# Attention scores by matmuls over 128 rows only: a two-layer encoder trunk on one Trainium2 core

## The chip, the cores and the metric

The program runs on one core of one Trainium2 chip. The core has a matmul engine (TensorE, PE in the profile, with its weight loads as PEld), three engines for elementwise work (VectorE or DVE, ScalarE or ACT, GpSimd or POOL), a queue that issues most of the transfers (SyncE, SP), and 16 DMA engines. The metric is device time in microseconds (us) from the first to the last instruction of the program; lower is better.

## The reference, cut to what matters

The input is a sequence of 2,048 tokens with 1,024 features, float32. Two layers follow each other. The first has two attentions side by side: a dilated one (A, 8 heads of 64 features) and a differential one (B, 4 heads, each with two score matrices, over all positions). The second has a banded grouped-query attention (C, 16 query heads, 4 key heads, keys within 128 positions).

```python
def differential_attention(q1, q2, k1, k2, v, lam, lam_init, subln_g):
    ...
        def attn(q, k):
            qs = lax.dynamic_slice_in_dim(q, start, Q_BLOCK, axis=2)
            s = jnp.einsum('bhqd,bhkd->bhqk', qs, k, preferred_element_type=jnp.float32) * scale + bias
            return jax.nn.softmax(s, axis=-1)

        a = attn(q1, k1) - lam * attn(q2, k2)
        return jnp.einsum('bhqk,bhkd->bhqd', a, v32)
...
def even_mixer(h, w_in, w_out, lq1, lk1, lq2, lk2, subln_g, lam_init):
    ...
    proj = h @ w_in
    ...
    return (y * jax.nn.silu(g)) @ w_out
```

A layer is: norm, `h @ w_in`, attention, a gate, `@ w_out`. All products are to be as good as float32.

## The kernel before, in words

**Two parts.** The matmuls take a rounded format, float32r. To keep float32's accuracy each operand is split into a high part and a low part that together hold it, and a product is the sum of high x high, high x low and low x high (`three`, three matmuls of 128 rows). Scores are products over the 64 features of a head, so 128 rows hold both parts of one operand at once. `scores` uses that: its first matmul, over 128 rows, has q's high and low part in the two halves and k's high part in both halves, and gives (q high + q low) k high. Its second, over the 64 rows where q's high part lies, adds q high x k low. The two write one PSUM tile, one right behind the other where nothing comes between. The columns of one matmul are keys: 512 in B, 256 or 512 or 384 in A, 384 (256 at the ends) in C.

**Stages.** In order: projections for B (`layer0_proj`); differential attention (`diff_head`, one call to a head, 8 steps of two query blocks of 128); dilated attention (`dil_pair`, two heads of 64 features to a pair; each head is done in the tokens' order, `dil_natural`, and by residue class mod 4, `dil_classes`); the first layer's output projection, run together with the second layer's first block; banded attention (`attend`, one call to a block of 128 queries, 16 in all), between which the second layer's projections lie; the second layer's gate and output projection.

**Fill.** Projections that are due later are written down as filling work beside the attentions: those of A (tiles `pp_a`, `pn_a`) beside B, the first layer's gate (`pp_g`) beside B and A, part of its output projection (`po0b`) beside A, the second layer's projections and gate (`pp_l`, `pn_l`, `pp_g`) beside C. Which instruction stands where on an engine is decided when the program is built, by a scheduler that runs its own estimate of the program; the engines then keep that order. So an edit to `scores` can shift the whole order.

**Names of the scores' tiles.** PSUM `pq` (B), `pqn` and `pqc` (A, natural and by class), `pqC` (C). Parts of k: `kBh` (high, both halves) and `kBl` (low) in B; `kn`/`kln`, `kc`/`klc` in A; `khC`/`klC` in C. After the scores VectorE adds the distance term and takes the maximum (lines 599, 777, 828, 1102), ScalarE takes the exponential, PE transposes, ScalarE and VectorE split the result in two parts (lines 626 and 627 in B), and PE multiplies by v (`py`, `pyn`, `pyc`, `pyC`).

**Queues.** Loads stand in SP's queue in the scheduler's order. A load into a buffer waits there until the buffer's last reader is done, and what is behind it waits as well. The tiles of v in C have 5 buffers (`vC`, tag `v`), k's high and low parts 2 each.

Of the kernel before, what the change touches and what calls it, by code (L numbers as in the profile page):

```python
# [37 lines left out]
def rsqrt(nc, pool, out, xin, name, iters=3):  # L38
    """out = xin ** -0.5 on VectorE: a first guess from the exponent, then Newton steps."""
# [18 lines left out]
class Bufs:  # L58
    """A pool with each tag's number of buffers."""
# [10 lines left out]
def tile_encoder(ctx: ExitStack, tc: tile.TileContext, x, c, ada_w, ada_b, norm_g, ab_w_in, ab_w_out,  # L70
# [38 lines left out]
    # ---------------------------------------------------------------- constants  # L109
# [12 lines left out]
    def small_consts(pool, ps):  # L122
        """Conditioning vector, lambda and the per-head norm's weights."""
# [28 lines left out]
    def ada_acc(pool, l, c0, name, raw=None):  # L152
        """Columns c0 .. c0 + 512: the sum over a partition's features of silu(c) * ada_w."""
# [19 lines left out]
    def ada_bias(ps, l):  # L173
        """ada_b's three parts and norm_g, a feature to a partition."""
# [42 lines left out]
    def ada_load(tiles, l, j):  # L217
        """The scale's and the shift's columns of ada_w to tiles[i][j], [128, KC, 512]."""
        for i in (1, 0):
            for n in range(2):  # L220
                c0, ks = i * D + j * 512, slice(n * KC // 2, (n + 1) * KC // 2)
                nc.sync.dma_start(tiles[i][j][:, ks],
                                  ada_w[l, :, c0:c0 + 512].rearrange("(k p) f -> p k f", p=P)[:, ks])

    # ---------------------------------------------------------------- norm + transposes
# [9 lines left out]
    def norm_block(pool, ps, l, b, xts, h):  # L235
        """512 tokens, normalised, to the features' layout: h[part][k] is [128, 512]."""
# [9 lines left out]
    def modulate(pool, l, name, src, k, h):  # L246
        """The conditioning's scale and shift, and the split into high and low parts."""
# [6 lines left out]
    # ---------------------------------------------------------------- input projections  # L254
    CH = 256

    def load_w(pool, w, c0, n, name, tag, eng=nc.vector):
        """Columns c0 .. c0 + n of w as high and low parts."""
# [12 lines left out]
    def three(pt, l, r, k, nk, after=None):  # L271
        """pt += (l0 + l1)^T (r0 + r1), less the product of the low parts."""
# [7 lines left out]
    def proj_T(pool, ps, w, c0, n, h, name, sink, wt, tick, blocks=range(TB)):  # L280
        """(h w)^T for columns c0 .. c0 + n (n <= CH), in pieces of 128 features x 512 tokens."""
# [10 lines left out]
    def proj_N(pool, ps, w, cols, n, h, name, sinks, tick):  # L292
        """h w for the n columns from each of cols, in pieces of 128 tokens x n features, block by block."""
# [12 lines left out]
    def proj_block(pool, ps, w, h, b, pieces, name, after=lambda b, n: None):  # L306
        """A block of 512 tokens by pieces of w: (first column, sink, None), 128 columns for (h w)^T,
        or (first column, None, sink), 256 columns for h w. h[part][k] is [128, 512]."""
# [27 lines left out]
    def split(pool, src, name, scale=1.0, shape=None):  # L336
        """The high and low parts of scale * src (in PSUM)."""
# [10 lines left out]
    def sink_heads(pool, dst, scale, name, classes=None):  # L348
        """A pair of 64-feature heads to dst(part, block), [128, 512]; classes(part): also by residue mod 4."""
# [13 lines left out]
    def pair(dst, h):  # L363
        """The parts of heads h and h + 1, a feature to a row."""
        return lambda i: dst[i, h:h + 2].rearrange("h f s -> (h f) s")
# [4 lines left out]
    def load_parts(q, src, h, cols, parity):  # L370
        """Head h's high parts to the first half of q and its low parts to the second, or the other way round."""
# [12 lines left out]
    def sink_v(pool, dst, dv, name, eng=nc.sync):  # L384
        """Heads of dv features, their high and low parts side by side."""
# [8 lines left out]
    # ================================================================ layer 0: norm, projections  # L394
    def load_x(pool, b, tag=None):
        """512 tokens; a tile to a pair of 128, or all in one of the tag's."""
# [23 lines left out]
    def layer0_proj(pool):  # L420
        with sbuf("pH", side="right") as hpool, psum("ps0", side="right") as ps0:
# [22 lines left out]
            # the first block waits in the second's place for the conditioning  # L444
# [9 lines left out]
            # what else is due, by the time passed in products (units of 128 x 128 x 256 x 24)  # L454
# [78 lines left out]
    # ================================================================ layer 0: differential attention  # L533
    def diff_attention(fill, psf, poolc):
        with sbuf("pB", side="right") as pool, psum("psB", side="right") as ps_:
            ps = Bufs(ps_, s=2, t=2, y=1)
            # -|k - q| by k - q; a head's slope (a power of two) is in q's scale and the exponential's
# [12 lines left out]
    NQ = 2                                            # query blocks that share a pass over V  # L550
    PB = 6

    def scores(ps_, q, kh, kl, a):
        """ps_ = q^T k less the product of the low parts; kh is in both halves, kl in half a."""
        first = nc.tensor.matmul(ps_, q, kh, start=True, stop=False)  # L555
        nc.tensor.matmul(ps_, q[a * 64:(a + 1) * 64], kl[a * 64:(a + 1) * 64], start=False, stop=True)  # L556
# [5 lines left out]
    def diff_head(pool, poolc, ps, h, ndist):  # L562
        def load_q(tp):
            q = pool.tile([P, 2, NQ * P], FR, name=f"q{h}_{tp}", tag="q", bufs=2)
            for a in range(2):
                load_parts(q[:, a], qB, 2 * h + a, slice(tp * NQ * P, (tp + 1) * NQ * P), a)
# [3 lines left out]
        KL = poolc.tile([P, S], FR, name=f"kBl{h}", tag="y2", bufs=1)  # L570
        KH = []
        for a in range(2):
            kt = pool.tile([P, S], FR, name=f"kBh{h}_{a}", tag="kh", bufs=2)
            for j in range(2):
                nc.sync.dma_start(f32(kt)[j * 64:(j + 1) * 64], kB[0, 2 * h + a])
            nc.sync.dma_start(f32(KL)[a * 64:(a + 1) * 64], kB[1, 2 * h + a])
# [669 lines left out]
```

## Time and profile before

| | |
|---|---|
| runs of the kernel before | median 3259.53 us of 3 (3256.40 to 3263.93) |
| the profiled execution, span | 3262.4 us |
| PE busy (matmuls) | 3110.2 us, 95% of the span, 14,992 matmuls |
| weight loads busy | 2323.1 us, 71% |
| DVE busy | 1915.4 us, 59% |
| ACT busy | 1494.5 us, 46% |
| POOL busy | 1141.3 us, 35% |
| transfers | 574.35 MB, mean 176 GB/s; the main queue's packets took 57.9% of 16 engines' span |
| mean granted TensorE clock | 0.968 of 2.4 GHz |

A matmul's row shows when it starts and a length whose end is modelled: successive matmuls overlap, so a busy PE need not be at its peak, and what tells the pace is the distance from one start to the next. "64\*128" in a row is the part of the array that the matmul uses, rows by columns; "64x512" is its moving operand.

### The profile page before, as it was taken

To read this page: it belongs to the slowest core of one execution; us is meant where nothing else is said; L and a number is where in the kernel's file an instruction comes from. 1 tells how busy PE (TensorE), PEld (TensorE's weight loads), DVE (VectorE), ACT (ScalarE), POOL (GpSimd) and SP (SyncE) were. 2 spreads that over 40 slices of the span, in tenths; PEclk is the share of its full clock that TensorE was granted. 3 is DMA by queue.
4 is the path that set the end of the run, shared out by engine and by line. 5 is a ranking of instruction groups with operands and counts; after the bars stand their busy time and mean duration, and the time that the engine had idled before them with its cause. 6 is when DMAs were issued, how large, how long until landed. Compare 5 with 4: busy or idle time off the path is not lost. (4 is left out here: it accounts for less than half of the span.)

```text
span 3262.4 us, 43544 instructions
## 1 busy us (share of the span) xinstructions
PE 3110.2 (95%) x14992; PEld 2323.1 (71%) x14992; DVE 1915.4 (59%) x4128; ACT 1494.5 (46%) x2841; POOL 1141.3 (35%) x755
## 2 busy tenths in 40 slices
PE   5999899999999999999999999799999999999998
PEld 4789667767767667677676776678767677777786
DVE  7434265665656656656565677653556665556476
ACT  4211245444544445444555666322456665555321
POOL 3200165454453544331242433232334343233221
PEclk8999799999999999999998999899999999999999
DMA  6677532542443444135867886686968666775654
GB/s 247 237 271 240 171 117 75 160 148 68 140 130 113 147 127 156 55 109 145 227 169 211 209 230 188 208 286 221 239 178 224 179 150 180 184 203 161 198 186 158
DMA packets 536246, 574.35 MB, mean 176 GB/s; under 512 B 31361, under 2 KB 406874, under 8 KB 529370
## 3 DMA queue, kind: packets, MB, share of 16 engines
q1 hardware_dynamic: 524186, 554.80, 57.9%
q10 hardware_dynamic: 11840, 16.78, 1.5%
q8 instruction: 118, 1.93, 0.3%
q14 instruction: 102, 0.84, 0.1%
HBM read 394.97 MB, written 176.46 MB: 175 GB/s over the span
## 5 line engine op out<-in xcount | busy, mean ns | idle before, releaser
L605 ACT ACTIVATE s<-s,nm 128x2048 f32<-128x2048 f32 x128 | 256.6, 2004 | 142.4 <-DVE nm L604 137.2
L626 ACT ACTIVATE th<-pt 128x512 fp32r<-128x512 f32 x256 | 148.2, 595 | 285.8 <-PE pt L622 247.8
L556 PE MATMUL pq<-kBl,q 64*128 64x512 f32 x512 | 259.5, 508 | 6.0 <-DMA kBl<-kB 6.0
L611 POOL TENSOR_SCALAR s<-s,rr 128x1536 f32<-128x1536 f32 x64 | 123.5, 1930 | 397.5 <-DVE rr L609 352.3
L627 DVE TENSOR_TENSOR tl<-pt,th 128x512 fp32r<-128x512 f32 x256 | 172.1, 686 | 146.3 <-ACT th L626 145.0
L555 PE MATMUL pq<-kBh,q 128*128 128x512 f32 x512 | 246.5, 482 | 7.6 <-DVE mx L599 5.6
L1102 DVE CUSTOM_DVE_ANT_0 sC<-pqC,tabC,isl 128x384 f32<-128x384 f32 (+1 forms) x256 | 150.8, 598 | 173.7 <-PE pqC L556 128.4
L599 DVE CUSTOM_DVE_ANT_0 s<-pq,ndist 128x1024 f32<-128x1024 f32 x128 | 156.3, 1221 | 159.7 <-PE pq L556 118.2
L614 POOL TENSOR_TENSOR s<-s,s 128x1536 f32<-128x1536 f32 x64 | 226.1, 3532 | 5.2
L599 DVE CUSTOM_DVE_ANT_0 s<-pq,ndist,mx 128x1024 f32<-128x1024 f32 x128 | 163.8, 1280 | 60.1 <-PE pq L556 58.4
L556 PEld LDWEIGHTS pq<-kBl,q 64*128 64x128 f32 x512 | 95.6, 188 | 138.2 <-issue 130.1
L1110 ACT ACTIVATE sC<-sC,nmC 128x384 f32<-128x384 f32 (+1 forms) x256 | 150.8, 592 | 58.3 <-DVE nmC L1107 58.1
L555 PEld LDWEIGHTS pq<-kBh,q 128*128 128x128 f32 x512 | 98.0, 192 | 89.9 <-issue 77.6
L276 PE MATMUL py<-tl,vB 128*128 128x256 f32 x512 | 155.6, 304 | 1.2 <-DVE tl L627 1.2
L622 PE MATMUL pt<-ident,s 128*128 128x128 f32 x1024 | 151.9, 275 | 2.5 <-DVE tl L627 2.5
L273 PE MATMUL py<-th,vB 128*128 128x256 f32 x512 | 151.2, 295 | 0.1
L315 POOL TENSOR_TENSOR wt_g<-wr_g,wt_g 128x1024 fp32r<-128x1024 f32 x32 | 76.8, 2400 | 199.5 <-ACT wt_g L314 196.8
L277 PE MATMUL py<-th,vB 128*128 128x256 f32 x512 | 145.7, 285 | 0.0
L1123 POOL TENSOR_SCALAR hC<-rC 128x512 fp32r<-128x512 f32 x64 | 40.1, 627 | 291.2 <-ACT rC L1122 269.8
L945 POOL TENSOR_TENSOR yr<-yr,gr 128x512 f32<-128x512 f32 (+1 forms) x46 | 59.5, 1297 | 209.5 <-DMA yr<-yT 58.9
L1116 PE MATMUL ptC<-ident,sC 128*128 128x128 f32 x736 | 131.9, 278 | 0.1
L273 PE MATMUL pp_l<-h1T,wt_l 128*128 128x512 f32 x320 | 129.1, 405 | 0.7 <-DVE vc L390 0.6
(415 smaller groups left out, 9244.3 us busy)
## 6 DMA issues: line engine op xcount, KB each, us to landing
wr_a<-in_ab_w_in_dram SPq DMA_DIRECT2D x48, 512.0 KB
wr_l<-in_c_w_in_dram SPq DMA_DIRECT2D x48, 512.0 KB
hD<-h0T SPq DMA_DIRECT2D x8, 2048.0 KB
aw_ss<-in_ada_w_dram SPq DMA_DIRECT2D x32, 512.0 KB
hs_a<-hD SPq DMA_DIRECT2D x16, 1024.0 KB
wr_g<-in_ab_w_in_dram SPq DMA_DIRECT2D x32, 512.0 KB
hs_g<-hD SPq DMA_DIRECT2D x16, 1024.0 KB
G<-gg_g SPq DMA_DIRECT2D x64, 256.0 KB
```

Of the source, the lines that this page charges most:

```text
L273: first = nc.tensor.matmul(pt, l[0], r[0], start=(k == 0), stop=False)
L276: nc.tensor.matmul(pt, l[0], r[1], start=False, stop=False)
L555: first = nc.tensor.matmul(ps_, q, kh, start=True, stop=False)
L556: nc.tensor.matmul(ps_, q[a * 64:(a + 1) * 64], kl[a * 64:(a + 1) * 64], start=False, stop=True)
L599: nc.vector.tensor_tensor_reduce(out=s_[:, half * 1024:(half + 1) * 1024], in0=pq, in1=ndist[:, o:o + 1024], scale=1.0, scalar=LOW if half ...
L605: nc.scalar.activation(s_, s_, AF.Exp, bias=nm, scale=slope_B(h), accum_out=lsum[:, a, t:t + 1])
L614: nc.gpsimd.tensor_tensor(Pm[0][:, W:], Pm[0][:, W:], Pm[1][:, W:], op=OP.add)
L622: nc.tensor.transpose(pt[:, kk, j], A[j][:, kb * P:(kb + 1) * P], ident)
L626: nc.scalar.activation(hi, src, AF.Copy)
L627: nc.vector.tensor_tensor(lo, src, f32(hi), op=OP.subtract)
L1102: nc.vector.tensor_tensor_reduce(out=s_[:, :n], in0=pq[:, :n], in1=tab[:, o:o + n], scale=1.0, scalar=isl[:, h:h + 1], op0=OP.add, op1=OP.max,
L1110: nc.scalar.activation(Sx[r][:, :n], Sx[r][:, :n], AF.Exp, bias=nm[:, h:h + 1], scale=slope_C(h), accum_out=ls[:, h:h + 1])
```

## The change: what it does

`scores` takes both operands of both matmuls from its caller, and both matmuls run over 128 rows. One operand of a pair holds its two parts in the two halves, the other is loaded to both halves, once with its high part and once with its low part. The two matmuls thus give all four products of the parts (before: three).

- B: k holds both parts in one tile (`kB`, high in the first half, low in the second; one tile to each of a head's two score matrices, one of them in a buffer of tag `kh`, which has 1 now, the other where `kBl` was). q is loaded twice, high part to both halves and low part to both halves (`q` has twice the size). The two matmuls of a pair have different weights and the same moving operand.
- A and C: q keeps its two parts in the halves; k's low part is loaded to both halves as its high part was. The two matmuls have the same weights. `klC` has twice the size, v in C 4 buffers for 5.

```diff
-    def scores(ps_, q, kh, kl, a):
-        """ps_ = q^T k less the product of the low parts; kh is in both halves, kl in half a."""
-        first = nc.tensor.matmul(ps_, q, kh, start=True, stop=False)
-        nc.tensor.matmul(ps_, q[a * 64:(a + 1) * 64], kl[a * 64:(a + 1) * 64], start=False, stop=True)
+    def scores(ps_, q0, k0, q1, k1):
+        first = nc.tensor.matmul(ps_, q0, k0, start=True, stop=False)
+        nc.tensor.matmul(ps_, q1, k1, start=False, stop=True)
         return first
...
-            q = pool.tile([P, 2, NQ * P], FR, name=f"q{h}_{tp}", tag="q", bufs=2)
+            q = pool.tile([P, 2, 2, NQ * P], FR, name=f"q{h}_{tp}", tag="q", bufs=2)
...
+                for j in range(2):
+                    nc.sync.dma_start(f32(q)[j * 64:(j + 1) * 64, a], qB[:, 2 * h + a, :, cols].rearrange("i f s -> f i s"))
...
+            kt = (pool.tile([P, S], FR, name=f"kB{h}_{a}", tag="kh", bufs=1) if a == 0 else
+                  poolc.tile([P, S], FR, name=f"kB{h}_{a}", tag="y2", bufs=1))
+            for i in range(2):
+                nc.sync.dma_start(f32(kt)[i * 64:(i + 1) * 64], kB[i, 2 * h + a])
...
-            nc.sync.dma_start(f32(KL)[mine, o:o + k1 - k0], kA[0][1, h, :, k0:k1])
+                nc.sync.dma_start(f32(KL)[j * 64:(j + 1) * 64, o:o + k1 - k0], kA[0][1, h, :, k0:k1])
...
-                    scores(pq[:, j], Q[:, c0:c0 + P], KH[:, c0:c0 + 256], KL[:, c0:c0 + 256], e)
+                    scores(pq[:, j], q, KH[:, c0:c0 + 256], q, KL[:, c0:c0 + 256])
...
-            nc.sync.dma_start(f32(KL)[mine], kA[1][1, h, :, cols])
+                nc.sync.dma_start(f32(KL)[j * 64:(j + 1) * 64], kA[1][1, h, :, cols])
...
-                V[u] = pool.tile([P, C_KV, P], FR, name=f"vC_{u}", tag="v", bufs=5)
+                V[u] = pool.tile([P, C_KV, P], FR, name=f"vC_{u}", tag="v", bufs=4)
...
-        KL = pool.tile([P, C_KV // 2, 384], FR, name=f"klC{t}", tag="kl", bufs=2)
+        KL = pool.tile([P, C_KV, 384], FR, name=f"klC{t}", tag="kl", bufs=2)
...
-                nc.sync.dma_start(f32(KL)[half, :, dst], kC[b][1, a::2, :, src].rearrange("h f s -> f h s"))
+                nc.sync.dma_start(f32(KL)[half, :, dst], kC[b][1, :, :, src].rearrange("h f s -> f h s"))
...
-                last = scores(pq[:, :n], Q[:, h], KH[:, kv, :n], KL[:, kv // 2, :n], kv % 2)
+                last = scores(pq[:, :n], Q[:, h], KH[:, kv, :n], Q[:, h], KL[:, kv, :n])
```

The scheduler's order shifts with it. On PE, in the dilated stage of the kernel before, at the scores of the fifth head's second class (`pqc_1_2`), matmuls of the gate's projection (`pp_g_3_7`) stand between the scores, the transposes (`ptc`) and the products with v (`pyc`):

```order
L273 MATMUL pp_g_3_7_18454<-hs_g_3_0_1_18198,wt_g_3_7_18451 128x512
L276 MATMUL pp_g_3_7_18454<-hs_g_3_1_1_18202,wt_g_3_7_18451 128x512
L555 MATMUL pqc_1_2_15176<-kc_1_15157,qc_1_15154 128x512
L556 MATMUL pqc_1_2_15176<-klc_1_15160,qc_1_15154 128x512
L277 MATMUL pp_g_3_7_18454<-hs_g_3_0_1_18198,wt_g_3_7_18451 128x512
L273 MATMUL pp_g_3_7_18454<-hs_g_3_0_1_18198,wt_g_3_7_18451 128x512
L276 MATMUL pp_g_3_7_18454<-hs_g_3_1_1_18202,wt_g_3_7_18451 128x512
L840 MATMUL ptc_0_3_15138<-ident,scl_0_1_15086 128x128
L840 MATMUL ptc_0_3_15138<-ident,scl_0_2_15092 128x128
```

At the same scores of the same head PE's order of the change has no filling work (line numbers are 2 higher in the changed file):

```order
L556 MATMUL pqc_1_0_15190<-kc_1_15182,qc_1_15179 128x384
L556 MATMUL pqc_1_1_15196<-kc_1_15182,qc_1_15179 128x512
L557 MATMUL pqc_1_0_15190<-klc_1_15183,qc_1_15179 128x384
L557 MATMUL pqc_1_1_15196<-klc_1_15183,qc_1_15179 128x512
L856 MATMUL pyc_0_15128<-ch_0_1_15134,vc_0_15102 128x512
L556 MATMUL pqc_1_2_15202<-kc_1_15182,qc_1_15179 128x512
L557 MATMUL pqc_1_2_15202<-klc_1_15183,qc_1_15179 128x512
L842 MATMUL ptc_0_3_15163<-ident,scl_0_1_15111 128x128
L842 MATMUL ptc_0_3_15163<-ident,scl_0_2_15117 128x128
```

Counted over the whole orders: between the first `pqn` and the last `pyc`, the order before has 384 matmuls of `pp_g` and 192 of `po0b`; the changed one has 72 of `pp_g`, of which 24 beside the first head, 24 in the last and 24 at its very end, and none of `po0b`. Of the others, 96 `pp_g` stand earlier, beside B, and 216 `pp_g` and all 192 `po0b` stand behind the last `pyc`. At that place PE's order before goes straight from the last products of the dilated stage to the output projection (`po`):

```order
L276 MATMUL po0b_1_18819<-wol0b,yh0b_4_18825 128x512
L277 MATMUL po0b_1_18819<-woh0b,yl0b_4_18826 128x512
L854 MATMUL pyc_3_17223<-ch_3_3_17262,vc_3_17197 128x384
L854 MATMUL pyc_3_17223<-cl_3_3_17263,vc_3_17197 128x384
L273 MATMUL po_0_0_18911<-woh0b,yh_0_4_18918 128x512
L276 MATMUL po_0_0_18911<-wol0b,yh_0_4_18918 128x512
```

and the changed one to what is left of the gate's projection:

```order
L856 MATMUL pyc_3_17275<-ch_3_3_17314,vc_3_17249 128x384
L856 MATMUL pyc_3_17275<-cl_3_3_17315,vc_3_17249 128x384
L273 MATMUL pp_g_2_7_18218<-hs_g_2_0_0_17960,wt_g_2_7_18215 128x512
L276 MATMUL pp_g_2_7_18218<-hs_g_2_1_0_17964,wt_g_2_7_18215 128x512
L277 MATMUL pp_g_2_7_18218<-hs_g_2_0_0_17960,wt_g_2_7_18215 128x512
```

On SP, the loads of the second block of banded attention stand in the same order in both; the kernel before loads k's low part for two heads to a half:

```order
L1077 DMA vC_20781<-vC_82 128x512
L1086 DMA khC_20783<-kC_78 64x4x384
L1087 DMA klC_20784<-kC_78 64x2x384
L1086 DMA khC_20783<-kC_78 64x4x384
L1087 DMA klC_20784<-kC_78 64x2x384
L1089 DMA qC_20785<-qC_74 64x16x128 x2
```

and the change for all four:

```order
L1079 DMA vC_20833<-vC_82 128x512
L1088 DMA khC_20835<-kC_78 64x4x384
L1089 DMA klC_20836<-kC_78 64x4x384
L1088 DMA khC_20835<-kC_78 64x4x384
L1089 DMA klC_20836<-kC_78 64x4x384
L1091 DMA qC_20837<-qC_74 64x16x128 x2
```

The order before changes between 64 and 128 rows 2,024 times, the changed one never.

## Rows read from the trace of the kernel before

**Rows 1.** Windows by stage: B, A, C (us; busy by engine, PEclk, DMA share, GB/s)

```profile
370.00:1504.00 1134.00, 1115.69 (x5477) 790.22 (x5478) 682.16 (x1248) 530.27 (x716) 518.61 (x231) 0.98 0.39 118
1504.00:2068.00 564.00, 536.67 (x2520) 391.08 (x2519) 378.79 (x986) 334.44 (x833) 190.78 (x186) 0.94 0.75 200
2315.00:3033.00 718.00, 710.92 (x3299) 519.19 (x3300) 420.43 (x1031) 411.24 (x949) 255.79 (x196) 0.98 0.70 187
```

**Rows 2.** PE's waits in B, longest in total first

```profile
PE pq L556 <- DMA kBl<-kB: 6.0, 5, 1.9
PE pq L555 <- DVE mx L599: 5.6, 4, 3.1
```

**Rows 3.** Timeline of PE in B: start, length, matmul

```profile
403.55 0.48 PE L555 MATMUL pq<-kBh,q 128*128 128x512 f32 x1
403.96 0.50 PE L556 MATMUL pq<-kBl,q 64*128 64x512 f32 x1
404.39 0.50 PE L555 MATMUL pq<-kBh,q 128*128 128x512 f32 x1
404.82 0.50 PE L556 MATMUL pq<-kBl,q 64*128 64x512 f32 x1
405.25 0.50 PE L555 MATMUL pq<-kBh,q 128*128 128x512 f32 x1
```

**Rows 4.** Timeline of PE in the last stage, no 64-row matmul near

```profile
3119.83 0.39 PE L273 MATMUL po<-woh1b,yh 128*128 128x512 f32 x1
3120.06 0.39 PE L276 MATMUL po<-wol1b,yh 128*128 128x512 f32 x1
3120.28 0.39 PE L277 MATMUL po<-woh1b,yl 128*128 128x512 f32 x1
3120.51 0.39 PE L273 MATMUL po<-woh1b,yh 128*128 128x512 f32 x1
```

**Rows 5.** Groups of PE by line and shape: every 64-row matmul

```profile
L556 PE MATMUL pq<-kBl,q 64*128 64x512 f32 x512 | 259.5, 508 | 6.0 <-DMA kBl<-kB 6.0
L556 PE MATMUL pqC<-klC,qC 64*128 64x384 f32 x224 | 98.7, 440 | 0.0
L556 PE MATMUL pqn<-kln,qn 64*128 64x256 f32 x128 | 49.5, 396 | 1.2 <-DMA kln<-kA 1.1
L556 PE MATMUL pqc<-klc,qc 64*128 64x512 f32 x64 | 33.2, 519 | 0.0
L556 PE MATMUL pqc<-klc,qc 64*128 64x384 f32 x64 | 29.5, 462 | 0.3 <-DMA klc<-kA 0.2
L556 PE MATMUL pqC<-klC,qC 64*128 64x256 f32 x32 | 13.4, 418 | 0.0
```

**Rows 6.** Groups of PE: 128-row matmuls of scores, and of a projection

```profile
L555 PE MATMUL pq<-kBh,q 128*128 128x512 f32 x512 | 246.5, 482 | 7.6 <-DVE mx L599 5.6 <-DMA kBh<-kB 2.0
L273 PE MATMUL pp_l<-h1T,wt_l 128*128 128x512 f32 x320 | 129.1, 405 | 0.7 <-DVE vc L390 0.6
```

**Rows 7.** Group of DVE: distance and maximum on a scores tile of B

```profile
L599 DVE CUSTOM_DVE_ANT_0 s<-pq,ndist,mx 128x1024 f32<-128x1024 f32 x128 | 163.8, 1280 | 60.1 <-PE pq L556 58.4
```

**Rows 8.** Windows of A: first head (no fill), second, last, all (as Rows 1)

```profile
1517.80:1569.30 51.50, 46.40 (x200) 30.75 (x198) 35.87 (x113) 31.50 (x85) 6.07 (x8) 0.87 0.78 203
1569.30:1650.00 80.70, 76.54 (x371) 57.34 (x372) 47.40 (x124) 47.48 (x113) 23.52 (x23) 0.98 0.78 220
...
1996.30:2067.70 71.40, 69.83 (x358) 52.19 (x357) 51.62 (x134) 44.62 (x114) 20.70 (x25) 1.00 0.55 165
...
1517.80:2067.70 549.90, 524.23 (x2468) 381.94 (x2467) 364.86 (x954) 329.59 (x824) 186.41 (x181) 0.94 0.74 200
```

**Rows 9.** PE's waits over the whole span

```profile
PE po L273 <- ACT yh L948: 16.3, 2, 16.0
...
PE pqn L555 <- DMA kn<-kA: 4.7, 2, 3.5
PE pqC L555 <- DMA qC<-qC: 3.5, 1, 3.5
```

**Rows 10.** Windows of PE at B's start (us; busy, PEclk, DMA share, GB/s)

```profile
376.00:400.00 24.00, 21.78 (x33) 0.50 0.60 173
406.00:430.00 24.00, 24.00 (x91) 1.00 0.44 132
```

More of the change, by code (lines that the diff above doesn't have):

```diff
@@ L563, in load_q @@
         def load_q(tp):
-            q = pool.tile([P, 2, NQ * P], FR, name=f"q{h}_{tp}", tag="q", bufs=2)
+            q = pool.tile([P, 2, 2, NQ * P], FR, name=f"q{h}_{tp}", tag="q", bufs=2)
+            cols = slice(tp * NQ * P, (tp + 1) * NQ * P)
             for a in range(2):
-                load_parts(q[:, a], qB, 2 * h + a, slice(tp * NQ * P, (tp + 1) * NQ * P), a)
+                for j in range(2):
+                    nc.sync.dma_start(f32(q)[j * 64:(j + 1) * 64, a], qB[:, 2 * h + a, :, cols].rearrange("i f s -> f i s"))
             return q
         Q0 = load_q(0)
-        KL = poolc.tile([P, S], FR, name=f"kBl{h}", tag="y2", bufs=1)
-        KH = []
+        K = []
         for a in range(2):
[L573 to L576, printed above, removed]
-            KH.append(kt)
+            kt = (pool.tile([P, S], FR, name=f"kB{h}_{a}", tag="kh", bufs=1) if a == 0 else
+                  poolc.tile([P, S], FR, name=f"kB{h}_{a}", tag="y2", bufs=1))
+            for i in range(2):
+                nc.sync.dma_start(f32(kt)[i * 64:(i + 1) * 64], kB[i, 2 * h + a])
+            K.append(kt)
         V = pool.tile([P, NT, 2, 128], FR, name=f"vB{h}", tag="v")
@@ L595, in diff_head @@
                             k0 = half * 1024 + n * 512
-                            scores(pq[:, n * 512:(n + 1) * 512], Q[:, a, j * P:(j + 1) * P],
-                                   KH[a][:, k0:k0 + 512], KL[:, k0:k0 + 512], a)
+                            k, cols = K[a][:, k0:k0 + 512], slice(j * P, (j + 1) * P)
+                            scores(pq[:, n * 512:(n + 1) * 512], Q[:, a, 0, cols], k, Q[:, a, 1, cols], k)
                         o = half * 1024 - t * P + (S - P)
@@ L741, in dil_natural @@
         vsrc = vA[:, h].rearrange("t i d -> t (i d)")
-        mine = slice(e * 64, (e + 1) * 64)
         for g in range(NT // 4):
@@ L752, in dil_natural @@
                 nc.vector.tensor_copy(KH[:, :64], z[:, :64])
-                nc.vector.tensor_copy(KL[mine, :64], z[mine, :64])
+                nc.vector.tensor_copy(KL[:, :64], z[:, :64])
                 nc.vector.tensor_copy(V[:64, 0], z[:64, :P])
@@ L758, in dil_natural @@
                 nc.vector.tensor_copy(KH[:, 576:], z[:, :64])
-                nc.vector.tensor_copy(KL[mine, 576:], z[mine, :64])
+                nc.vector.tensor_copy(KL[:, 576:], z[:, :64])
                 nc.vector.tensor_copy(V[64:, 4], z[64:, :P])
@@ L775, in dil_natural @@
                     c0 = (2 * b + j) * P
-                    scores(pq[:, j], Q[:, c0:c0 + P], KH[:, c0:c0 + 256], KL[:, c0:c0 + 256], e)
+                    q = Q[:, c0:c0 + P]
+                    scores(pq[:, j], q, KH[:, c0:c0 + 256], q, KL[:, c0:c0 + 256])
                     nc.vector.tensor_tensor_reduce(
@@ L807, in dil_classes @@
         vsrc = vA[:, h].rearrange("(b p r) i d -> r p b (i d)", p=P, r=4)
-        mine = slice(e * 64, (e + 1) * 64)
         for r in range(4):
@@ L813, in dil_classes @@
             KH = pool.tile([P, 512], FR, name=f"kc{h}_{r}", tag="kc", bufs=2)
+            KL = pool.tile([P, 512], FR, name=f"klc{h}_{r}", tag="klc", bufs=2)
             for j in range(2):
                 nc.sync.dma_start(f32(KH)[j * 64:(j + 1) * 64], kA[1][0, h, :, cols])
-            KL = pool.tile([P, 512], FR, name=f"klc{h}_{r}", tag="klc", bufs=2)
-            nc.sync.dma_start(f32(KL)[mine], kA[1][1, h, :, cols])
+                nc.sync.dma_start(f32(KL)[j * 64:(j + 1) * 64], kA[1][1, h, :, cols])
             V = pool.tile([P, 4, P], FR, name=f"vc{h}_{r}", tag="vc", bufs=2)
@@ L824, in dil_classes @@
                 s_ = pool.tile([P, 512], F32, name=f"scl{h}_{r}_{b}", tag="p", bufs=6)
-                scores(pq[:, :n], Q[:, b * P:(b + 1) * P], KH[:, lo_k:lo_k + n], KL[:, lo_k:lo_k + n], e)
+                q = Q[:, b * P:(b + 1) * P]
+                scores(pq[:, :n], q, KH[:, lo_k:lo_k + n], q, KL[:, lo_k:lo_k + n])
                 o = lo_k - b * P + 384
```

## The prediction

> **What bounds the kernel now.** I read the windows by stage first. In all three attentions PE is busy nearly throughout: 1115.7 of 1134 us in B, 536.7 of 564 in A, 710.9 of 718 in C; the next engine, VectorE, has 60%, 67% and 59%, and the transfers come near their limit in A alone (share 0.75) and C (0.70) [rows 1]. The waits confirm it: PE's longest in B are 6.0 and 5.6 us in total [rows 2]. So what PE's stream loses or gains shows in the span until another engine catches up.
>
> Then the timeline, because busy time does not tell PE's pace. Where no 64-row matmul is near, matmuls of 512 columns start every 0.23 us [rows 4]. Where 64-row and 128-row matmuls alternate they start every 0.41 to 0.43 us, and the 128-row ones are as late as the 64-row ones [rows 3]. No wait stands there, the columns are the same, and in both places each matmul has a weight load of its own and adds to the PSUM tile that the one before it wrote. What differs is that the number of rows changes at each step. So a change of rows costs time, in both directions.
>
> **What the change removes: 2,024 changes of rows.** There are 512 + 224 + 128 + 64 + 64 + 32 = 1,024 matmuls over 64 rows [rows 5]; in the order before they make 2,024 changes (12 times two of them stand together), in the order after none. The price of one, in a run: 0.43 - 0.23 = 0.20 us [rows 3, 4]. It is less where the 64-row matmul comes behind a 128-row one that was itself not delayed. Reading every step of the trace in the way of these rows, without those at half clock or above 0.7 us (a wait), the mean step into a 64-row matmul is 0.156 us longer (957 steps) and that out of one 0.196 us longer (956) than a step of the same columns without a change. That makes 1,012 x 0.352 = 356 us. Bounds: all at the price of a run, 1,024 x 0.40 = 410 us; by the rows' own lengths, 508 + 482 - 2 x 405 = 180 ns to a matmul [rows 5, 6], 184 us, but these ends are modelled, so I take the starts. By stage, with the stage's own means: B 507 x 0.368 = 187 us, A 249 x 0.344 = 86 us, C 256 x 0.328 = 84 us.
>
> The number of matmuls and their columns stay: the second one of a pair has twice the rows and streams the same columns, 0.23 us at 512. The added product of the low parts is free in this sense.
>
> **B: 187 us, less what VectorE can't follow.** The scheduler puts 96 more `pp_g` beside B: 96 x 0.23 = 22 us more to do there. And a cover goes: a scores tile of 1,024 columns took four matmuls x 0.43 = 1.72 us, longer than VectorE's 1.28 us on it [rows 3, 7]; now it takes 0.92 us, and there are two PSUM buffers for it. Where tiles stand back to back PE waits for VectorE. If all 256 did, that is 256 x 0.36 = 92 us; in the order after 67 tiles follow the one before by less than 1.3 us of PE's work, and lack 24 us together. Below is nothing. I take 25 us. VectorE as a whole has 682 us for a stage that PE needs some 970 for, so it does not bind on average. B: 1134 - 187 + 22 + 25 = 994 us.
>
> Loads of B: q's grow by 128 x 64 KB = 8.4 MB, k's shrink by 4.2 MB (a head loads 2 MB, not 3), at a DMA share of 0.39 [rows 1]; nothing. The single `kh` buffer makes no new wait: each of a head's k tiles waited for the scores of the head before already, and `kBl`, which both score matrices read, was the longest [rows 2].
>
> **A: from PE to the transfers.** Here the order matters more than the price of a change. Seven of eight heads lose their fill. What a head without fill takes is to be seen in the first one: 51.5 us [rows 8], of which PE is busy 46.4, with 64 changes of rows, some 11 us. Without these PE would need about 40 us. VectorE has 35.9 and ScalarE 31.5 us of work in it. The transfers: share 0.78 of 51.5 us is 40.2 us for 10.4 MB (51.5 us x 203 GB/s) [rows 8], 3.9 us to a MB. The doubled low parts of k add four loads of about 0.15 MB and four of 0.13, 1.1 MB or 4.3 us: 44.5 us. So a head can't fall much below 44.5 us, and 51.5 us is its upper end; I take 46, nearer to the lower one since the changes of rows were on PE's own path. The last head runs out with nothing behind it and took 71 us [rows 8], 19 us of it `po0b` (84 matmuls x 0.23): 52. A: 7 x 46 + 52 = 374 us, for 550 before (1517.8 to 2067.7, with the fill) [rows 8].
>
> The fill that left does not vanish: 216 `pp_g` and 192 `po0b` behind A, 408 x 0.23 = 94 us, dense. There they cover something: before, PE stood 16.0 us where the output projection began, waiting for the last heads' results to come back from DRAM [rows 9], with a stretch of half clock behind it. I take 20 us back. A and what follows: 550 - (374 + 94) + 20 = 102 us less.
>
> **C: 84 us, less waits for loads.** k's low part adds 6 MB to 134 (718 us x 187 GB/s), 3.7 us to a MB: 23 us of transfer time in a stage of about 640 us whose share was 0.70 [rows 1]; about 0.83, no bound on average. The load of v now takes the buffer of one block later and waits on SP for the products of the block before last; behind it stand k and q of the next block. At some 40 us to a block it still comes early, mostly. The nearest row is a wait for q, 3.5 us [rows 9]: none to 16 x 3.5 = 56 us; I take 20. C: 718 - 84 + 20 = 654 us.
>
> **Sum.** B -140, A and behind it -102, C -64: 306 us less. The profiled execution has 3262.4 us, 2.9 above the median of the runs shown, so the same 306 from the median gives 3254; I make the sum against the profile and forecast 3262 - 306 = 2956 us, 9% less.
>
> **The rivals.**
> *PE stays the bound everywhere* (0.13). Then all 356 us and the 20 behind A come out: 2886 us. For it: waits of a few us in each stage today [rows 2, 9]. Against it: the first head of A, full of transfers and bare of fill.
> *The others catch up further* (0.22): A's heads stay at 51.5 us (+44), B's tiles all wait (+67), C's loads too (+36): 3103 us with all three, about 3030 with half of each.
> *Nothing is removed* (0.03). If a 64-row matmul and a 128-row one cost the same and the slow steps in B come from something that the pair keeps, say two matmuls that read other tiles, the span stays at 3262 us. Against it: other pairs that change both tiles run at 0.23 us [rows 4]. The Trainium skill ("TensorE: Matmul & The Clock Gate", section "Why this matters for your kernels") has a rule of this kind: a matmul over few rows takes as long as one over all 128, and what can be gained from few rows is to run several side by side in different row groups. By that rule alone widening gives nothing and the sum is 3262 us; the trace differs, since here the time lies in the step between two row counts, 0.20 us, and not in the rows.
> *Slower* (0.02): PE's clock. At half the clock PE starts 33 matmuls in 24 us, at the full one 91 of a similar mix [rows 10], and A's bare first head had a mean grant of 0.87 with PE waiting now and then, a filled one 0.98 [rows 8]. If the bare heads wait often, stretches at 1.2 GHz give the gain back: a stretch costs half its length. To lose 306 us it takes 612 us more of them, all of A and a quarter of B; below that it only trims. The Trainium skill, same page and section, warns of this: gaps between bursts of matmuls bring the half clock.
>
> **The numbers.** Forecast's case 0.60, with its own range from 2915 to 3000 us. The range reaches from the full gain to the case in which two of the three allowances are near their upper ends: 2885 to 3065 us. This kernel can tell 0.2%, some 6.5 us, from no change. Faster 0.95 (all cases but the last two); within 0.2%, 0.02; slower 0.03, from the clock and from part of the third, in which the added loads cost something.
>
> **What would show it.** Steps of 0.23 us in runs of `pq`; matmul rows over 128 rows alone, the two of a pair equal in length and near 0.40 us. B in about 990 us, new waits of `pq` on VectorE's maximum of 20 to 30 us. Heads of A some 46 us apart, a DMA share near 0.95 there, PE below 85% busy, and no 16 us wait at the start of `po`. C near 655 us. I am wrong if steps of scores stay near 0.4 us, if heads of A take over 52 us, or if the mean clock falls below 0.92.

## The result: 3.3% faster, a third of what was forecast, and the profile after

Change: median 3155.54 us of 4 runs (3146.60 to 3157.49). Kernel before beside it: 3261.73 us. Ratio 0.9667, 95% interval 0.9649 to 0.9686. Forecast were 2956 us and a range of 2885 to 3065: the direction was right, the size was not.

The profiled execution has a span of 3155.7 us, so 106.7 less than before. Where they lie, cut at the starts of the first and last matmuls of each stage (us), beside what the prediction made of each:

| stretch | before | forecast | after | after less forecast |
|---|---|---|---|---|
| start to the first `pq` | 370.3 | 370.3 | 382.3 | +12.0 |
| B, first `pq` to last `py` | 1133.4 | 993.4 | 981.7 | -11.7 |
| between B and A | 14.1 | 14.1 | 17.4 | +3.3 |
| A, first `pqn` to last `pyc` | 549.9 | 374 | 446.5 | **+72.5** |
| behind A, to the first `pp_l` | 113.5 | 187.5 | 290.2 | **+102.7** |
| to the first `pqC` | 134.4 | 134.4 | 136.5 | +2.1 |
| C, first `pqC` to last `pyC` | 717.7 | 654 | 673.6 | **+19.6** |
| to the end | 229.1 | 229.1 | 227.6 | -1.5 |

(187.5 is 113.5 as before, plus the 94 of the fill, less the 20 of cover.) The right column adds up to 199 us: all of the miss is in A, right behind it, and a little in C.

Windows of the change: B; A; A's second to fifth head; behind A; C (columns as in [rows 1], to which they answer).

```profile
382.30:1364.00 981.70, 941.69 (x5572) 813.40 (x5572) 680.05 (x1252) 531.37 (x724) 529.07 (x234) 0.98 0.50 149
1381.40:1827.90 446.50, 352.22 (x1965) 287.91 (x1963) 298.98 (x884) 296.25 (x781) 152.35 (x166) 0.90 0.76 191
1432.60:1484.20 51.60, 40.89 (x241) 34.56 (x240) 35.21 (x109) 36.11 (x98) 12.33 (x16) 0.90 0.74 181
1484.20:1542.00 57.80, 43.53 (x235) 35.87 (x235) 41.01 (x112) 37.79 (x101) 29.37 (x29) 0.88 0.77 189
1542.00:1586.90 44.90, 37.54 (x240) 31.01 (x240) 36.56 (x109) 36.14 (x99) 12.21 (x16) 1.00 0.78 205
1586.90:1652.00 65.10, 47.78 (x239) 39.53 (x240) 35.88 (x111) 38.73 (x101) 29.65 (x30) 0.82 0.74 180
1827.90:2118.10 290.20, 210.37 (x814) 160.52 (x815) 106.50 (x154) 50.40 (x74) 54.04 (x41) 0.88 0.60 193
2254.50:2928.10 673.60, 636.40 (x3304) 529.51 (x3304) 424.55 (x1031) 411.29 (x949) 254.36 (x195) 0.96 0.81 207
```

That a change of rows costs time was read rightly. The timeline of PE in B [rows 3] now has `pq` every 0.23 us, and its two groups [rows 5, 6] are nearly alike in length, 422 and 404 ns, where the 128-row ones had 482 with the same rows and columns:

```profile
405.39 0.40 PE L556 MATMUL pq<-kB,q 128*128 128x512 f32 x1
405.62 0.39 PE L557 MATMUL pq<-kB,q 128*128 128x512 f32 x1
405.85 0.39 PE L556 MATMUL pq<-kB,q 128*128 128x512 f32 x1
406.08 0.39 PE L557 MATMUL pq<-kB,q 128*128 128x512 f32 x1
```

```profile
L556 PE MATMUL pq<-kB,q 128*128 128x512 f32 x512 | 216.3, 422 | 25.8 <-DMA kB<-kB 12.8 <-DVE mx L601 11.8 <-DVE tl L629 0.7
L557 PE MATMUL pq<-kB,q 128*128 128x512 f32 x512 | 206.6, 404 | 0.0
```

The last columns of the first of these rows are B's new waits: 11.8 us for VectorE's maximum, 5.6 before [rows 2]; 25 were allowed.

What a change of rows costs shows in the weight loads (PEld). In the run of [rows 3] each load starts only with its own matmul (403.96 and 404.39 there):

```profile
403.95 0.18 PEld L556 LDWEIGHTS pq<-kBl,q 64*128 64x128 f32 x1 [0.25 <-issue]
404.39 0.19 PEld L555 LDWEIGHTS pq<-kBh,q 128*128 128x128 f32 x1 [0.25 <-issue]
```

In the change it starts while the matmul before is running, 0.23 us ahead of its own (405.62 and 405.85 above):

```profile
405.39 0.19 PEld L557 LDWEIGHTS pq<-kB,q 128*128 128x128 f32 x1
405.62 0.19 PEld L556 LDWEIGHTS pq<-kB,q 128*128 128x128 f32 x1
```

Over the whole trace of before, in steps at full clock and under 0.7 us: where the rows change, the load starts 1 to 3 ns ahead of its matmul in nine of ten of the 1,908 steps; where they don't, half of the 12,522 loads start 0.12 us ahead or more. So what the change of rows took away, and the kernel of the change has back, is the overlap of the weight load with the matmul before.

PE's waits behind A, longest in total first (us, times, longest):

```profile
PE po0b L273 <- DVE xo0b L971: 23.0, 13, 2.1
PE pp_g L273 <- DVE gg_g L380: 19.0, 8, 6.2
PE po0b L273 <- ACT yh0b L950: 10.1, 1, 10.1
PE po0b L273 <- ACT woh0b L921: 8.7, 3, 4.4
PE pp_g L273 <- DMA hs_g<-hD: 7.7, 1, 7.7
PE pp_g L276 <- DMA hs_g<-hD: 5.6, 1, 5.6
PE po L273 <- ACT yh L950: 2.8, 2, 2.3
```

The last row is the 16.0 us wait of before [rows 9], which is covered as forecast. The six above it are new. The timeline shows the first of them: a group of twelve matmuls at 0.23 us, then nothing until VectorE has read out the tile:

```profile
1995.23 0.47 PE L273 MATMUL po0b<-woh0b,yh0b 128*128 128x512 f32 x1 [2.08 <-DVE xo0b L971]
...
1997.59 0.39 PE L276 MATMUL po0b<-wol0b,yh0b 128*128 128x512 f32 x1
1997.82 0.39 PE L277 MATMUL po0b<-woh0b,yl0b 128*128 128x512 f32 x1
1999.72 0.50 PE L273 MATMUL po0b<-woh0b,yh0b 128*128 128x512 f32 x1 [1.52 <-DVE xo0b L971]
```

### The profile page after: what moved, and what is told of

Its sections match the earlier page's. It is cut to its first block, busy times and chain, and to the rows that moved or that the text cites. A ratio compares the mean times of both kernels' runs of the same rounds, so it can differ in the third digit from the quotient of the medians.

```text
span 3155.7 us, 43735 instructions
## 1 busy us (share of the span) xinstructions
PE 2813.2 (89%) x14992; PEld 2353.4 (75%) x14992; DVE 1898.2 (60%) x4128; ACT 1486.8 (47%) x2841; POOL 1138.1 (36%) x755
## 5 line engine op out<-in xcount | busy, mean ns | idle before, releaser
L556 PE MATMUL pq<-kB,q 128*128 128x512 f32 x512 | 216.3, 422 | 25.8 <-DMA kB<-kB 12.8
L557 PE MATMUL pq<-kB,q 128*128 128x512 f32 x512 | 206.6, 404 | 0.0
L629 DVE TENSOR_TENSOR tl<-pt,th 128x512 fp32r<-128x512 f32 x256 | 169.4, 683 | 58.0 <-ACT th L628 57.8
L556 PEld LDWEIGHTS pq<-kB,q 128*128 128x128 f32 x512 | 98.8, 193 | 55.2 <-DVE mx L601 21.6
L273 PE MATMUL pp_g<-hs_g,wt_g 128*128 128x512 f32 x256 | 106.1, 415 | 31.5 <-DVE gg_g L380 22.2
L277 PE MATMUL pp_l<-h1T,wt_l 128*128 128x512 f32 x320 | 127.7, 401 | 6.2 <-POOL wt_l L315 5.4
L273 PE MATMUL pp_l<-h1T,wt_l 128*128 128x512 f32 x320 | 128.4, 402 | 1.6 <-DVE vc L390 1.4
```

The lines of the kernel that those rows point to most:

```text
L273: first = nc.tensor.matmul(pt, l[0], r[0], start=(k == 0), stop=False)
L277: nc.tensor.matmul(pt, l[1], r[0], start=False, stop=(k == nk - 1))
L556: first = nc.tensor.matmul(ps_, q0, k0, start=True, stop=False)
L557: nc.tensor.matmul(ps_, q1, k1, start=False, stop=True)
L629: nc.vector.tensor_tensor(lo, src, f32(hi), op=OP.subtract)
```

## The experiments

Eleven kernels ran. My theory after the result: the changes of rows were priced rightly, and what came back is (1) the doubled loads of k in A, by themselves and by pushing the fill out of A, (2) the fill behind A, which has one PSUM buffer and so can't be dense, (3) A's heads, sized from the first one. The rivals are in the expectations. In the diffs - is the change unless something else is said; `mine` is the half with q's high part.

**e1: A over 128 rows with single loads.** k's low part goes to one half, beside zeros that stand for good in the other half of two tiles for each of A's two forms; q has its high part in the first half for every head. The products are those of the kernel before.

```diff
-            load_parts(Q, qA[0], h, blk(g), e)
+            load_parts(Q, qA[0], h, blk(g), 0)
...
-            KL = pool.tile([P, 640], FR, name=f"kln{h}_{g}", tag="kln", bufs=2)
+            KL = C["kz"][0][g % 2]
...
-                nc.sync.dma_start(f32(KL)[j * 64:(j + 1) * 64, o:o + k1 - k0], kA[0][1, h, :, k0:k1])
+            nc.sync.dma_start(f32(KL)[:64, o:o + k1 - k0], kA[0][1, h, :, k0:k1])
```

> B and C as in the change, A's scores over 128 rows too, but k's low part is loaded to one half alone, beside zeros that stay in the other half: no change of rows anywhere, and A's loads as in the kernel before. In its order the fill lies in A again (288 pp_g and 192 po0b), none behind. Theory (the doubled loads push the fill out of A, and that costs what the change lacks): A and what follows up to the first pp_l take 663 us before less 86 for the changes of rows and 22 for the 96 pp_g that moved to B, 555 us, for 737 in the change; the whole 3155 - 180 = about 2975 us. Rival one (bare heads and the fill behind would cost the same wherever the fill stands, since A is bound by its own latency): 3100 to 3155 us. Rival two (zeros or another order bring a new wait): slower than 3155 us.

Measured: 3032.50 us, ratio 0.9308 (0.9275 to 0.9341), 123 us below the change, where the theory said 180 and rival one at most 55. Its order has 288 `pp_g` and all 192 `po0b` in A and none behind. Windows of A and of what follows:

```profile
1375.00:1874.10 499.10, 422.12 (x2372) 351.86 (x2371) 353.08 (x952) 320.81 (x816) 177.61 (x179) 0.94 0.77 206
1874.10:1994.90 120.80, 97.35 (x406) 76.01 (x407) 63.53 (x91) 26.01 (x39) 33.35 (x28) 0.90 0.75 237
```

619.9 us for the two, 736.7 in the change. A is shorter than in the kernel before by 51 us and not by the 108 that I expected (442). A new wait, for another load, accounts for part of that; the rest stays open.

```profile
PE pqn L556 <- DMA kn<-kA: 28.1, 7, 8.7
```

**e2 and e3: A as before, and A as before with the change's loads.** Both have B and C of the change and A's second matmul over 64 rows; e2 loads k's low part once, e3 to both halves.

```diff
-                    scores(pq[:, j], q, KH[:, c0:c0 + 256], q, KL[:, c0:c0 + 256])
+                    scores(pq[:, j], q, KH[:, c0:c0 + 256], q[mine], KL[mine, c0:c0 + 256])
```

> B and C as in the change, A as before, with 64-row matmuls and single loads. The fill lies in A (288 pp_g, 192 po0b). Theory: A and what follows take 663 - 22 = 641 us for 737 in the change, so A's own part of the change costs some 95 us and the whole is about 3060 us. Rival (A's part of the change gains, and what it lacks comes from elsewhere, as from B's or C's loads): 3155 us or more.

> As the change, but A's second matmul of each pair over 64 rows; k's low part is still loaded to both halves. The order has the fill where the change has it (72 pp_g in A, 216 pp_g and 192 po0b behind). Theory (the bare heads follow loads and the chain of engines, not PE): the heads of A take some 55 us as in the change, a few more at most, the whole 3155 to 3195 us. Rival (PE still paces the bare heads): 86 us more, 3240 us.

Measured: e2 3068.17 us, 0.9421 (0.9391 to 0.9450); e3 3193.93 us, 0.9805 (0.9768 to 0.9842). The loads alone, with the same matmuls, cost 126 us. In its order, and in the time behind A, e3 is like the change: 72 `pp_g` in A, 294.0 us behind it (A itself takes 492.3); e2 has all its fill in A and 120.5 us behind. So it is the loads that push the fill out, not the 128 rows. In A the change of rows is worth 3193.9 - 3155.5 = 38 us with doubled loads and, e2 to e1, 36 us with single ones. The whole of e3 lies at the upper end of what the theory said.

**e4, e6, e7: one stage's part alone** (A, B, C), the other two as before; the edits are the change's own hunks for the stage.

> The kernel before with A's part of the change alone (128 rows and doubled loads in A; B and C over 64 rows). The order has 72 pp_g in A and 312 pp_g and 192 po0b behind it. Theory: A and what follows take about 446 + 290 + 30 = 766 us for 663 before: slower than before, 3262 + 100 = about 3360 us. Rival (the changes of rows in A are worth more than the fill's place costs): 3262 or less; by the prediction's sum 3262 - 100 = 3160 us.

> B's part of the change alone; A and C over 64 rows with single loads. By the change's own B stage (982 us for 1133, with 96 pp_g more) and 641 us for A and what follows, less 22 + 152 us: 3262 - 174 = about 3088 us. Rival (part of what B gains goes back in A, as the loads come closer together there): 3110 to 3130 us.

> C's part of the change alone. By the change's own C stage (674 us for 718): about 3218 us; by the prediction's term of C, 64 us, 3198 us; by the changes of rows alone, 84 us, 3178 us.

Measured: A alone 3380.01 us, 1.0373 (1.0332 to 1.0414), **slower** than before; B alone 3117.84, 0.9547 (0.9528 to 0.9566); C alone 3216.48, 0.9854 (0.9835 to 0.9874). Against the kernel before as it ran beside them (3259.89, 3263.49, 3263.49) that is +120, -146 and -47: -73 in sum, for -106 together. B's part alone beats the whole change. In e4's profile A and what follows take 765.8 us, for 663.4 before; 322.6 of them lie behind A, for 290.2 in the change, since without B's part 96 `pp_g` more land there. e6 missed its theory (3088 us) and lies in the range of its rival, though not for the rival's reason: A takes 530.5 us, 19 less than before; what is lost lies behind it (123.3 us, 10 more) and in C (730.0 us, 12 more, with C's code as before). Why is open.

**e5: more PSUM buffers for the fill behind A.** Behind A each group takes the fill's own buffer or one of A's three for transposes, in turn.

```diff
+    class Alt:
...
+            if "pp_g" in name and int(name.split("_")[2]) * 8 + int(name.split("_")[3]) < 22 or self.n % 4 == 0:
+                return self.one.tile(shape, dt, name, tag=tag, bufs=bufs)
+            return self.other.tile(shape, dt, name, tag="t")
...
-        layer0_gate_proj(fill, psf)
+        layer0_gate_proj(fill, Alt(psf, ps_))
...
-        layer0_out(pool, psG, w, [upper], g, x, x0d, "0b", "mm", range(FULL, HALF))
+        layer0_out(pool, Alt(psG, ps_A), w, [upper], g, x, x0d, "0b", "mm", range(FULL, HALF))
```

> The change, but the fill behind A writes to four PSUM buffers in turn (its own one and A's three for transposes) where it had one. The order keeps 196 pp_g and 192 po0b behind A. Theory (with one buffer each group of the fill waits until VectorE has read the group before; in the change 22 us of pp_g on gg_g and 23 us of po0b on xo0b, and the half clock that comes of it): the part behind A goes from 290 to about 235 us, the whole to about 3100 us. Rival (the loads of the fill, hs_g, w_out, yT and G, pace it): 3140 to 3156 us.

Measured: 3103.87 us, 0.9507 (0.9482 to 0.9533), 52 us below the change. The window behind A, and its longest waits:

```profile
1820.30:2060.40 240.10, 196.19 (x796) 152.75 (x795) 109.24 (x152) 48.60 (x72) 58.56 (x41) 0.91 0.69 228
```

```profile
PE po0b L273 <- ACT yh0b L960: 12.0, 3, 10.6
PE po L273 <- ACT yh L960: 7.5, 2, 4.8
PE pp_g L276 <- DMA hs_g<-hD: 6.5, 1, 6.5
```

290.2 us have become 240.1, some 5 of the 50 because 20 `pp_g` fewer stand there, and the two waits for VectorE (23.0 and 19.0 us) are no longer among the longest, with A itself as long as in the change (442.2 us, for 446.5). What stays waits for operands that were loaded or split late.

**e9: e1 with the fill held behind A.** The gate's last eleven pieces of 32 (264 matmuls) wait for A's last product, and the 192 `po0b` come behind them; 24 `pp_g` are left in A.

```diff
-        layer0_gate_proj(fill, psf)
+        layer0_gate_proj(fill, psf, lambda b, n: C["last"] if 8 * b + n >= 21 else None)
```

> As e1 (128 rows everywhere, A's loads single), but the gate's projection from its 22nd piece on is held back behind the last product of A, so that A's heads are bare as in the change (24 pp_g in A; 264 pp_g and 192 po0b behind). It parts the loads' direct price from the price of the fill's place. If the loads pace a bare head (the prediction's step, 3.9 us to a MB): heads of about 55.8 - 4.3 = 51.5 us, A's stage 412 us for 446, the part behind near 300 us, the whole about 3125 to 3135 us. If the chain through the engines paces it: heads and stage as in the change, the whole about 3160 us. Either way far from e1's 3032 us if the place of the fill is what costs.

Measured: 3125.73 us, 0.9585 (0.9556 to 0.9615). So the place of the fill alone costs 3125.7 - 3032.5 = 93 us of the 123 that lie between e1 and the change, and what else the doubled loads do some 30 (e9 holds 48 `pp_g` more behind A than the change does, so the parting is not exact). The window of A, shorter than either theory had it:

```profile
1376.90:1775.70 398.80, 327.46 (x1917) 268.27 (x1915) 303.70 (x888) 293.82 (x779) 152.54 (x165) 0.94 0.72 188
```

That is 398.8 / 8 = 49.9 us to a head, and 446.5 / 8 = 55.8 in the change, which however has 72 `pp_g` in A for 24. Heads two to seven have none in either kernel: (1763.9 - 1432.6) / 6 = 55.2 us in the change, (1721.9 - 1430.3) / 6 = 48.6 here. So the doubled loads cost 6.6 us a head, where 4.3 were forecast.

**e8 and e11: C's loads and its buffer.** Both are e1 with C's second matmul over 64 rows and v in 4 buffers; e8, shown here, keeps the doubled loads of k's low part, e11 has those of before.

```diff
-                last = scores(pq[:, :n], Q[:, h], KH[:, kv, :n], Q[:, h], KL[:, kv, :n])
+                mine = slice(kv % 2 * 64, kv % 2 * 64 + 64)
+                last = scores(pq[:, :n], Q[:, h], KH[:, kv, :n], Q[mine, h], KL[mine, kv, :n])
```

> As e1, but C's second matmul of a pair over 64 rows, with k's low part still loaded to both halves and four buffers for v. It parts C's changes of rows from its loads. If the doubled loads and the buffer cost the 40 us that C's stage lacks: C's stage 718 + 40 = 758 us, the whole about 3115 us. If they cost nothing while PE is slower, and the 40 us come of the other engines once PE is faster: C's stage 718 us, the whole about 3076 us.

> The kernel of e1 with C as before (the second matmul of a pair over 64 rows, k's low part loaded once, two heads to a half), but v with 4 buffers. Beside e8 (736 us in C, with the doubled loads too) it tells the loads from the buffer. Theory 'loads': C takes about 720 us as before, the kernel 3075 us. Rival 'buffer': C takes about 736 us as in e8, the kernel 3090 us.

**e10: e1, and C too with single loads beside standing zeros.** v keeps 4 buffers. (Against e1.)

```diff
-        KL = pool.tile([P, C_KV, 384], FR, name=f"klC{t}", tag="kl", bufs=2)
+        KL = kzC[t % 2]
...
-                nc.sync.dma_start(f32(KL)[half, :, dst], kC[b][1, :, :, src].rearrange("h f s -> f h s"))
+            nc.sync.dma_start(f32(KL)[:64, :, dst], kC[b][1, :, :, src].rearrange("h f s -> f h s"))
```

> The kernel of e1, and in C too k's low part is loaded to one half alone, beside zeros that stand in two tiles klC of their own, while q keeps its high part in the first half for every head. All matmuls of scores are over 128 rows, v has 4 buffers as in e1, and the 6 MB of doubled loads in C are gone. Theory 'loads' (what C lacked of its gain are the doubled loads): C takes some 655 us for 674, the kernel 3015 us. Rival 'buffer' (it is v's fifth buffer, or VectorE and GpSimd that PE now waits for): C stays within 5 us of 674, the kernel at 3030 us.

Measured: e8 3088.15 us, 0.9456 (0.9435 to 0.9477); e11 3073.82, 0.9425 (0.9402 to 0.9449); e10 3018.76, 0.9254 (0.9229 to 0.9280), the fastest of all. The window of C in each, e8:

```profile
2131.10:2866.80 735.70, 719.07 (x3299) 523.68 (x3300) 418.94 (x1031) 411.85 (x949) 254.75 (x196) 0.97 0.74 190
```

e11:

```profile
2127.80:2849.50 721.70, 712.92 (x3292) 520.10 (x3293) 427.07 (x1031) 412.46 (x949) 255.15 (x196) 0.98 0.70 186
```

e10:

```profile
2123.60:2782.80 659.20, 628.77 (x3301) 526.13 (x3302) 420.18 (x1032) 410.30 (x949) 256.65 (x197) 0.97 0.78 203
```

and e1, with 128 rows and the doubled loads:

```profile
2129.70:2803.90 674.20, 635.08 (x3300) 530.70 (x3301) 414.61 (x1031) 410.53 (x949) 257.81 (x196) 0.96 0.81 207
```

The doubled loads cost 735.7 - 721.7 = 14 us with 64 rows and 674.2 - 659.2 = 15 with 128 (e1 less e10), and the kernels' medians say the same (14.3 and 13.7): the theory of the loads holds. e8 itself lies between its own two cases, 758 and 718. The fifth buffer of v shows no price: with it, and C's code as before, the stage took 717.7 us (before), 725.4 (e4) and 730.0 (e6), without it 721.7. The change of rows gave 721.7 - 659.2 = 62, or 735.7 - 674.2 = 61 with doubled loads.

## Why the prediction was right in direction and wrong in size

**Changes of rows: right, and counted a little low.** Steps of 0.23 us, equal lengths, B 11.7 us shorter than forecast. PE's idle time in B went from 18 us to 40 (windows above and [rows 1]), so 151.7 less in the stage, 22 of added fill and 22 of idle time make 196 us that have left PE's work, for 187 forecast. The count of 356 us left a part out: the step right behind a change is late too, although its own rows don't change. At 512 columns and full clock it takes 0.34 us, from one 128-row matmul to the next (305 steps) and from one 64-row matmul to the next (3 steps). So each change costs 0.10 us in its own step and 0.10 in the one behind it, which makes 0.43 where each step is both; the steps left out come to 24 us in B, 18 in A and 20 in C. The 25 us of lost cover were too many: 11.8. That B starts 12 us later was not forecast; in the nine experiments that have B's part it starts 2 to 7 us later than before, in the two without (e4, e7) less than 1, and the cause stays open. In the first table the two cancel.

**"Nothing is removed": fell.** By the Trainium skill ("TensorE: Matmul & The Clock Gate", section "Why this matters for your kernels") a matmul over few rows takes as long as one over 128, and by that alone e6 should stand at 1.00. It stands at 0.9547. For the rows alone the trace agrees: the 0.34 us from one 64-row matmul to the next and from one 128-row matmul to the next, each behind a change, are the same. The rule says nothing of the change between two row counts, and that is where these 146 us lay.

**Failed: "408 x 0.23 = 94 us, dense".** The fill took its place behind A and cost 176.7 us there (290.2 - 113.5), with the cover given back in it. The price of 0.23 us is that of matmuls between which PE always has something else. The fill has one PSUM buffer (`psG = Bufs(..., mm=1)`, line 1163): inside A a group's result is read out while PE works on scores; alone, each next group waits for the readout. PE is idle there for 290.2 - 210.4 = 79.8 us; before it was for 21 (113.5 - 92.3), 16 of them the wait that went. The rows of waits give 42.0 us to the one buffer (`xo0b`, `gg_g`) and 32.1 to late loads and splits (`yh0b`, `woh0b`, `hs_g`). e5 took the former away: of its 50 us, 36 are idle time (79.8 to 43.9). The rest of the miss is pace. The window of the kernel before behind A (columns as in [rows 1]):

```profile
2067.70:2181.20 113.50, 92.34 (x408) 73.62 (x406) 64.42 (x91) 26.47 (x39) 33.71 (x28) 0.92 0.81 258
```

The change has 406 matmuls more there and 118 us more of busy time, 0.29 us each and not 0.23, at a granted clock of 0.88 for 0.92: 406 x 0.06 = 24 us.

**Failed: "What a head without fill takes is to be seen in the first one".** The prediction took 46 us; the heads took 55.8. Two things were put at nothing. The 72 `pp_g` that the order leaves in A were added neither there nor behind it: 72 x 0.23 = 17 us. And the first head is not like the others, because it opens the first pair of heads. Heads three, five and seven each open a pair too, and have the combination of the pair before beside them (`dil_combine`): sixteen loads `F`, 128 KB each, and GpSimd's work on them, 29 us for the 12 of heads that close a pair (windows above). Less 46 us each, these three (57.8, 65.1, 64.5) are 49 us too long together, heads two, four and six (51.7, 44.9, 47.4) 6 us, and the first and the last (less 46 and 52), which hold the 72, 17 us. On SP half of the `F` stand right before a load of v, and PE waits for that load once in each of the three heads, 14.5 us together. In head five:

```profile
1602.35 5.23 SPq L902 DMA_DIRECT2D F<-fA  x8
1607.69 1.56 SPq L765 DMA_DIRECT2D vn<-vA  x1
1613.47 2.90 PE L799 MATMUL pyn<-pn,vn 128*128 128x256 f32 x12 [4.93 <-DMA vn<-vA]
```

The granted clock was 0.82 to 0.88 in these three heads and 0.90 to 1.00 in the three that close a pair. How the rest divides among `F`, GpSimd and the clock was not separated. The first head's window is also short of matmuls, since the last of them stand in the next head's window: 200 [rows 8], for 235 to 241 in the bare heads of the change. That is not what cost: in e4, whose first two heads have no fill, the first took the 46 us of the forecast with 200 matmuls, and the second as much with 242 (columns as in [rows 1]):

```profile
1514.00:1559.50 45.50, 36.91 (x200) 28.52 (x200) 35.22 (x113) 30.94 (x84) 6.09 (x8) 0.92 0.85 221
1559.50:1605.90 46.40, 39.84 (x242) 32.52 (x242) 36.48 (x110) 36.14 (x98) 12.36 (x16) 0.96 0.77 201
```

So 46 us was right for the first head, and for heads that close a pair nearly so. One head's window is no sharp ruler, though: in e7, with A's code as before, the first head took 58.0 us at a clock of 0.76, for 51.5 at 0.87 [rows 8]. The loads added 6.6 for 4.3 (e9), most of it in the heads that open a pair (there 53.8, 50.6, 52.8). What I feared of the transfers did not come: their share is 0.76, not 0.95. They are late one by one, as PE's waits in A show:

```profile
PE pyn L799 <- DMA vn<-vA: 14.5, 3, 5.4
PE pqn L557 <- DMA kln<-kA: 7.5, 6, 4.5
...
PE pqc L556 <- DMA kc<-kA: 6.7, 7, 2.4
PE pqc L557 <- DMA klc<-kA: 6.6, 9, 2.4
```

**The order was seen and mispriced.** That A would lose its fill stood in the order. Why it does so I had not asked; e1 to e3 answer it: the doubled loads do it. The rows of SP's queue for the gate's weights (first and last issue) before, after and in e1:

```profile
L312 SPq DMA_DIRECT2D wr_g<-in_ab_w_in_dram x32: 373/384/4679, 1256.6 to 1806.2; - x32
```

```profile
L312 SPq DMA_DIRECT2D wr_g<-in_ab_w_in_dram x32: 367/384/1491, 1111.0 to 1894.3; - x32
```

```profile
L312 SPq DMA_DIRECT2D wr_g<-in_ab_w_in_dram x32: 373/384/939, 1104.4 to 1485.2; - x32
```

In the change the last weights are asked for 66 us after A's last product (1827.9): the last eleven of the 32 stand where A's own loads end, from 1801 us on. In the other two all come before A is over. By what rule the scheduler put them there was not tried. The prediction set 176 us less in A, and 20 of cover, against the fill's 94 and found a gain of 102; the profile shows 73 us of loss over both stretches (736.7, for 663.4), and e4, alone, the same sign.

**C: a term mis-sized.** 84 us were priced (104 with the steps left out), 62 came; in the change's C PE waits for `mxC` (8.9 us), `lC` (8.8), `qC` (6.7) and a weight (5.4), for 1.2, 1.4, 3.5 and none before. How the missing 22 divide among them was not separated. Loads and buffer were allowed 20; the loads cost 14 to 15, and the buffer shows no price.

**The rivals.** "The others catch up further" came nearest and had A's heads at 51.5 as its worst; the heads took more, and it had no price for the fill behind A. The clock rival only trimmed: 0.953 for 0.968 over the span, 0.88 behind A. In the two traces 299 us of the span are at half clock, for 213 before, 86 more; at half a stretch's length that is 43 us at most. The two windows of [rows 10] are no measure of it, since their mix is not alike: 30 of the 33 matmuls are B's scores, but 27 of the 91.

## What to carry to other kernels

Look for the distance from one matmul's start to the next where matmuls over different numbers of rows alternate: 0.43 for 0.23 us was worth 146 us in B alone, though PE was 98% busy; fill up the rows, and where the second copy would cost a load, use zeros that stand there for good. Price filling work by the place where it lands: what is free between other matmuls runs with one PSUM buffer at the pace of its readout when it stands alone. A stage's first unit is a bad ruler for the others where a unit carries work of the one before; look in its window for what the later ones do besides.

## What the runs showed of the hardware that was not expected

- Between two matmuls of different rows the next weights were not loaded ahead: the load started 1 to 3 ns before its matmul, where otherwise half of the loads started 0.12 us ahead or more. Each change cost 0.10 us in its own step and 0.10 in the step behind it.
- Eight more small loads a head cost more through the order than by their own time: 126 us in e3, with the same matmuls as e2, and 93 us by the fill's place alone (e9 less e1). In the change's A the DMA share is 0.76 over the stage, and PE waits for its loads all the same.
- e10 and e11 have nearly the same number of matmuls in C's window (3,301 and 3,292) and, but for 7 us of VectorE, 2 of ScalarE and 2 of GpSimd, the same work on the other engines; PE is busy for 712.9 of 721.7 us with 64-row matmuls among the others, and for 628.8 of 659.2 without. A stage that PE filled to 99% had 62 us in it that neither a busy share nor a wait showed.
